# Moving the subtraction that makes the low part of a split weight from GpSimd to VectorE

## Chip, core and metric

The kernel runs on one core of one Trainium2 chip. The metric is the device time of one execution in microseconds (us). Engines are named as the profile names them: PE (TensorE matmul), PEld (TensorE weight load), DVE (VectorE), ACT (ScalarE), POOL (GpSimd), SP (SyncE, which here issues the DMAs).

## What is computed

One step of a two-layer streaming encoder on 2048 prompt frames and 32 sample frames of width 1024. Layer 0 is a sliding-window grouped-query attention with sinks and ALiBi, layer 1 a gated DeltaNet. Cut to what matters here:

```python
for i in range(2):
    h = rmsnorm(x, norm_g[i])
    if i == 0:
        q, k, v, gate = split(h @ attn_w_in)          # 20 blocks of 128 columns
        o = softmax_with_sink(q @ k.T - alibi) @ v    # 64-frame chunks, 128 frames back
        x = x + (o * silu(gate)) @ attn_w_out         # 8 blocks of 128 columns
    else:
        ...                                           # gated DeltaNet: dn_w_in, dn_w_out
y = rmsnorm(x, final_norm_g)
```

All of it is in float32. The projections keep that accuracy on faster matmuls by splitting each operand in two: `hi` is the operand rounded to the type fp32r, `lo` is the operand minus `hi`. A product is then three matmuls: hi·hi, hi·lo and lo·hi.

## The kernel before

**Work and stages.** The tokens lie in four slabs of 512 columns (the second has 544, with the 32 sample frames, and is worked as two groups of 272). In the attention layer each slab goes through 20 blocks of the input projection (`wa`) and 8 of the output projection (`wao`, method `out_blocks`, block number f = 0 to 7). A block is 128 output features: per group of columns 8 input tiles times 3 matmuls, 24 in a row into one bank of the accumulator `pj`, which has two banks. The profile shows this layer from 0 to about 945 us of the span; the DeltaNet layer follows.

**Weights of the attention layer.** Class `Weights` loads a block as two halves (`wr`, 128x512 each, three buffers). `split` then makes, half by half, `hi` by a cast on ACT and `lo` by a subtraction (`low`), each into a tile `wh`. There are six buffers of `wh`, taken in turn; a block uses four of them in the order hi, lo, hi, lo. A new `wh` therefore has to wait until PE has finished with the sixth `wh` before it.

**Weights of the DeltaNet layer.** During the attention of the first two slabs, `keep_ahead` splits all 41 blocks of the later layer once: load half a block (`pr`, two buffers), cast to `ph` on ACT, store `ph` to HBM, subtract in place (`low`), store `pr`. The DeltaNet layer then only loads ready parts (`wh<-xswwd`), so nothing of the change is executed in it.

**Attention.** `attend` handles one pair of heads and 256 frames: scores on PE into two banks `ta`; on DVE the bias is added and the maximum taken (`s<-ta,bias`, `mx`), then three small operations (`mx`, `es`, `mx`); exponentials on ACT; on DVE the sum `den`, its reciprocal and four scalings `s<-s,den`; transposes on PE (`tb`), copies on ACT (`pt`), the product with v on PE (`tc`), the gate on DVE (`of`), and a split of the result (cast on ACT, subtraction on POOL: `hk<-of`).

**Output blocks.** The accumulated block is evacuated by one DVE addition per group, `xr<-pj,xr`, which adds the residual that was loaded into `xr` (two buffers); the sum is stored to HBM.

**Order.** Every instruction is recorded first and issued later by a list scheduler (`Order.flush`). It holds a cost for each operation on each engine (`Estimate.COST`: DVE 68 ns + 1.04 ns an element, POOL 140 + 2.14) and issues on each engine what it believes to be ready, in order of recording. After that the order on each engine is fixed: an engine works its list strictly in order, and an instruction that waits holds up everything behind it. All operations are issued by one helper, so that the profile shows line 185 for each; tiles tell them apart.

Of the kernel before, what the change touches and what calls it, by code (L numbers as in the profile page):

```python
# [12 lines left out]
F32R = mybir.dt.float32r  # L13
# [338 lines left out]
class Weights:  # L352
# [23 lines left out]
    def split(self, free):  # L376
        kern = self.kern
        there = lambda x: free == KT or kern.est.write[x.tensor.name][0] <= kern.clock
        while len(self.lo) < len(self.halves):
            i = len(self.hi)  # L380
            half = self.halves[i if i < len(self.halves) else -1]
            if self.kept is not None:
                if free != KT and free < 4 * i:
                    return
                for made, part in ((self.hi, 0), (self.lo, 1)):
                    made.append(self.place(len(half)))
                    kern.nc.sync.dma_start(
                        made[-1].bitcast(F32), self.kept[half[0] // 4][part][:, half[0] % 4 : half[-1] % 4 + 1, :])
            elif i > len(self.lo) and there(self.hi[-1]):
                self.lo.append(self.place(len(half)))  # L390
                kern.low(self.raws[i - 1], self.hi[-1], self.lo[-1], kern.nc.gpsimd)
            elif i == len(self.lo) and (free == KT or free >= 4 * i) and there(self.raws[i]):
                self.hi.append(self.place(len(half)))
                kern.nc.scalar.copy(self.hi[-1], self.raws[i])
            else:
                return


class Kern:
# [25 lines left out]
    def keep_ahead(self, srcs):  # L425

        nc = self.nc
        todo = [(src, h) for src in srcs for h in range(2)]

        def load(src, h):  # L430
            raw = self.t(self.ap, [P, 4, P], "pr", bufs=2)
            nc.sync.dma_start(raw, self.weight(src)[:, 4 * h : 4 * h + 4, :])
            return raw

        def put(src, h, part, x):
            name = f"w{src[0]}{src[1]}_{h}{part}"
            place = self.dp.tile([P, 4, P], F32, tag=name, name=SCRATCH + name)
            nc.sync.dma_start(place, x)
            return place

        nxt = load(*todo[0])
        for i, (src, h) in enumerate(todo):
            raw, nxt = nxt, load(*todo[i + 1]) if i + 1 < len(todo) else None
            yield raw
            hi = self.t(self.ap, [P, 4, P], "ph", F32R, bufs=1)
            nc.scalar.copy(hi, raw)
            yield hi
            parts = [put(src, h, 0, hi.bitcast(F32))]
            self.low(raw, hi, raw.bitcast(F32R), nc.gpsimd)
            yield raw  # L450
            parts.append(put(src, h, 1, raw))
            self.keeping.setdefault(src, []).append(parts)
            if h:
                self.kept[src] = self.keeping[src]
            yield 4500
# [1797 lines left out]
```

## Time and profile before

| what | before |
|---|---|
| median of 3 runs | 2376.36 us (2372.67 to 2381.98) |
| the profiled execution | 2376.4 us |
| its span, first to last instruction | 2374.6 us |
| mean granted TensorE clock | 0.978 |
| busy in the span: PE, DVE, ACT, POOL | 95%, 69%, 53%, 36% |
| subtractions `wh<-wr,wh` on POOL | 224, 295.5 us |
| subtractions `pr<-pr,ph` on POOL | 82, 111.8 us |

A row of the groups names line, engine, operation, output<-inputs, shapes, count, then busy us and mean ns of one, then the idle time of the engine just before and what ended it. A row of the timeline gives start (us), duration (us), engine, operation, count, and in brackets the idle time before it and who ended that. A row of the windows gives the stretch, its length, the busy us of PE, PEld, DVE, ACT and POOL (with counts), the granted clock, the DMA share and GB/s. A row of the waits says which engine waited before which tile, for whom, for how long in total, how often, and the longest.

### The profile page before, as it was taken

How to read it: one execution, taken by the hardware profiler on the slowest of the kernel's cores; microseconds unless marked ns; L12 is line 12 of the kernel's file. 1: busy time of each engine (PE TensorE's matmuls, PEld its weight loads, DVE VectorE, ACT ScalarE, POOL GpSimd, SP SyncE). 2: the span in 40 equal slices, each digit the busy share in tenths (PEclk: the TensorE clock that was granted, in tenths of full speed). 3: DMA queues.
4: the chain of work that ended last, by engine and by line, in shares of the span. 5: the costliest groups of instructions: out<-in, count | busy, mean ns of one | idle time of the engine just before them, and what ended most of it. 6: DMA issues, size and time to landing. Idle time of an engine off the chain costs nothing.

```text
span 2374.6 us, 44457 instructions
## 1 busy us (share of the span) xinstructions
PE 2252.8 (95%) x14759; PEld 1843.9 (78%) x14759; DVE 1639.6 (69%) x5024; ACT 1262.2 (53%) x3792; POOL 862.9 (36%) x1044
## 2 busy tenths in 40 slices
PE   8998999999999999999999999989999999999997
PEld 5777788797778777777778788877798767777776
DVE  6765465626553445588887768889786888876876
ACT  5555466636553554455566354564644466445533
POOL 4556555665554334222322121331312222122222
PEclk9998999999999999999999999999999999999998
DMA  7556755585434115544423664333456634466442
GB/s 253 175 187 192 255 188 181 174 279 190 147 105 150 62 63 159 193 149 140 143 89 126 200 227 136 128 115 122 147 172 215 200 118 138 134 215 216 155 142 67
DMA packets 222832, 382.75 MB, mean 161 GB/s; under 512 B 29922, under 2 KB 45194, under 8 KB 222602
## 3 DMA queue, kind: packets, MB, share of 16 engines
q1 hardware_dynamic: 220154, 377.75, 49.4%
q8 instruction: 116, 1.90, 0.3%
q10 hardware_dynamic: 2448, 2.16, 0.3%
q14 instruction: 114, 0.93, 0.1%
HBM read 311.63 MB, written 68.19 MB: 160 GB/s over the span
## 4 chain that ended last, share of the span: by engine, by line
PE 56%; DVE 28%; ACT 7%; issue 4%; DMA 3%; POOL 2%; SPq 0%; DVEq 0%; ACTq 0%; POOLq 0%
PE pj L185 39%; PE tb L185 6%; PE ta L185 5%; PE tc L185 4%; DVE cy L185 4%; DVE s L185 3%; DVE sub L185 3%; DVE tl L185 3%; ACT s L185 2%; DVE ml L185 2%; ACT ta L185 1%; DVE xa L185 1%; DVE r L185 1%; DVE md L185 1%; DVE mx L185 1%
## 5 line engine op out<-in xcount | busy, mean ns | idle before, releaser
L185 PE MATMUL pj<-hk,wh 128*128 128x512 f32 (+1 forms) x8184 | 1770.1, 364 | 26.9 <-DVE xr L185 8.6
L185 PEld LDWEIGHTS pj<-hk,wh 128*128 128x128 f32 x8184 | 1326.6, 191 | 237.9 <-issue 14.1
L185 POOL TENSOR_TENSOR wh<-wr,wh 128x512 fp32r<-128x512 f32 x224 | 295.5, 1321 | 328.2 <-ACT wh L185 283.7
L185 DVE SCALAR_TENSOR_TENSOR cy<-cx,cw,cy 128x512 f32<-128x512 f32 x360 | 230.6, 651 | 44.7 <-ACT cy L185 41.1
L185 ACT CAST wh<-wr 128x512 fp32r<-128x512 f32 x224 | 138.1, 618 | 203.6 <-PE pj L185 157.3
L185 ACT ACTIVATE s<-s,mx 128x256 f32<-128x256 f32 (+1 forms) x272 | 132.0, 487 | 30.1 <-DVE mx L185 29.9
L185 ACT ACTIVATE qs<-tb,egq 64x128 f32<-64x128 f32 x264 | 95.7, 362 | 89.7 <-DVE r L185 76.5
L185 DVE TENSOR_TENSOR sub<-ml,tl 128x60 f32<-128x60 f32 (+24 forms) x527 | 125.8, 239 | 10.2
L185 DVE TENSOR_SCALAR s<-s,den 128x256 f32<-128x256 f32 (+1 forms) x272 | 130.9, 530 | 1.2
L185 ACT ACTIVATE cx<-cy 128x512 f32<-128x512 f32 (+1 forms) x96 | 61.1, 636 | 130.9 <-DVE cy L185 101.5
L185 DVE TENSOR_TENSOR tl<-tl,sub 128x60 f32<-128x60 f32 (+24 forms) x527 | 122.3, 232 | 10.1
L185 DVE CUSTOM_DVE_ANT_0 s<-ta,bias 128x256 f32<-128x256 f32 (+1 forms) x272 | 95.7, 405 | 43.5 <-PE ta L185 42.9
L185 POOL TENSOR_TENSOR pr<-pr,ph 128x512 fp32r<-128x512 f32 x82 | 111.8, 1364 | 34.9 <-ACT ph L185 28.8
L185 POOL COPY cx<-hist 128x3 f32<-128x3 f32 x96 | 25.5, 265 | 263.9 <-DVE kq L185 63.6
L185 DVE TENSOR_TENSOR xr<-pj,xr 128x512 f32<-128x512 f32 (+1 forms) x72 | 41.2, 577 | 112.1 <-PE pj L185 70.1
L185 POOL TENSOR_TENSOR so<-so,mhalf 128x4 f32<-128x4 f32 x33 | 36.8, 1115 | 216.9 <-DVE so L185 189.1
L185 DVE SCALAR_TENSOR_TENSOR r<-tb,nbk,vb 64x128 f32<-64x128 f32 x264 | 91.7, 348 | 29.6 <-PE tb L185 25.1
L185 ACT ACTIVATE qs<-o 128x128 f32<-128x128 f32 x132 | 40.7, 308 | 133.8 <-DVE o L185 128.3
L185 ACT COPY cx<-pj 128x512 f32<-128x512 f32 (+2 forms) x149 | 64.1, 445 | 77.5 <-PE pj L185 62.1
L185 PE MATMUL tb<-st,kq 128*128 128x128 f32 x512 | 94.7, 286 | 6.8 <-DVE st L185 5.9
L185 PEld LDWEIGHTS tb<-st,kq 128*128 128x128 f32 x512 | 82.9, 194 | 21.5 <-DVE st L185 13.0
L185 PE MATMUL tb<-con,s 128*128 128x128 f32 (+2 forms) x528 | 77.7, 280 | 18.9 <-DVE s L185 16.0
(242 smaller groups left out, 3558.0 us busy)
## 6 DMA issues: line engine op xcount, KB each, us to landing
wh<-xswwd SPq DMA_DIRECT2D x528, 256.0 KB
wr<-in_wa SPq DMA_DIRECT2D x160, 256.0 KB
wh<-xswwdo SPq DMA_DIRECT2D x112, 256.0 KB
pr<-in_wd SPq DMA_DIRECT2D x66, 256.0 KB
xswwd<-ph SPq DMA_DIRECT2D x66, 256.0 KB
xswwd<-pr SPq DMA_DIRECT2D x66, 256.0 KB
wr<-in_wao SPq DMA_DIRECT2D x64, 256.0 KB
xa<-in_x SPq DMA_DIRECT2D x48, 256.0 KB
```

The lines of the kernel that those rows point to most:

```text
L185: self.order.add(Op(self.name, lambda: call(*args, **kw), cost, op == "dma_start"), ins, outs)
```

## The change

Both calls of `low` on weights name VectorE instead of GpSimd:

```diff
@@ Weights.split
-                kern.low(self.raws[i - 1], self.hi[-1], self.lo[-1], kern.nc.gpsimd)
+                kern.low(self.raws[i - 1], self.hi[-1], self.lo[-1], kern.nc.vector)
@@ Kern.keep_ahead
-            self.low(raw, hi, raw.bitcast(F32R), nc.gpsimd)
+            self.low(raw, hi, raw.bitcast(F32R), nc.vector)
```

`low` itself stays `eng.tensor_tensor(out=lo, in0=src, in1=hi.bitcast(F32), op=ALU.subtract)`. 306 instructions change their engine. The scheduler books them with DVE's cost and orders the attention layer anew on every engine; the DeltaNet layer keeps its order on all of them.

The first place is in slab 0, in an `attend` of the input blocks. On DVE before, its four scalings (`s_245`) and the gate products around them:

```order
L185 TENSOR_TENSOR den_247<-den_247,es_248 128x4
L185 RECIPROCAL den_247<-den_247 128x4
L185 TENSOR_SCALAR s_245<-s_245,den_247 128x256 x4
L185 SCALAR_TENSOR_TENSOR of_272<-tc_269,sg_233 128x256
L185 TENSOR_TENSOR sg_279<-pj_260,rb_169 128x512
L185 SCALAR_TENSOR_TENSOR of_284<-tc_278,sg_233 128x256
```

On POOL before, what stands about the same point:

```order
L185 TENSOR_TENSOR wh_267<-wr_258,wh_261 128x512
L185 TENSOR_TENSOR wh_270<-wr_259,wh_268 128x512
L185 TENSOR_TENSOR pr_314<-pr_314,ph_351 128x512
L185 TENSOR_TENSOR hk_273<-of_272,hk_273 128x256
L185 TENSOR_TENSOR wh_292<-wr_281,wh_285 128x512
```

On DVE now:

```order
L185 TENSOR_TENSOR den_247<-den_247,es_248 128x4
L185 RECIPROCAL den_247<-den_247 128x4
L185 TENSOR_SCALAR s_245<-s_245,den_247 128x256 x4
L185 TENSOR_TENSOR wh_267<-wr_258,wh_262 128x512
L185 TENSOR_TENSOR wh_271<-wr_259,wh_268 128x512
L185 TENSOR_TENSOR pr_314<-pr_314,ph_349 128x512
L185 SCALAR_TENSOR_TENSOR of_272<-tc_270,sg_231 128x256
```

The two subtractions on `wh` and the one on `pr` now stand behind the four scalings, in front of the gate product.

The second place is the output projection of slab 0 (`xr` is the evacuating addition of a block, `acc` a sum of squares). On DVE before, the additions of blocks f = 2, 3 and 4:

```order
L185 TENSOR_TENSOR xr_663<-pj_674,xr_663 128x512
L185 TENSOR_TENSOR acc_665<-acc_665,sq_688 128x512
L185 TENSOR_TENSOR xr_673<-pj_687,xr_673 128x512
L185 TENSOR_TENSOR acc_665<-acc_665,sq_701 128x512
L185 TENSOR_TENSOR xr_686<-pj_700,xr_686 128x512
```

On DVE now, from the addition of block 3 (`xr_663`) to that of block 4 (`xr_674`); `wh_708` and `wh_710` are the low parts of block 6, `wh_721` is that of block 7's first half:

```order
L185 TENSOR_TENSOR xr_663<-pj_675,xr_663 128x512
L185 TENSOR_TENSOR acc_654<-acc_654,sq_689 128x512
L185 TENSOR_TENSOR wh_708<-wr_698,wh_707 128x512
L185 TENSOR_TENSOR pr_831<-pr_831,ph_856 128x512
L185 TENSOR_TENSOR wh_710<-wr_699,wh_709 128x512
L185 TENSOR_TENSOR wh_721<-wr_711,wh_720 128x512
L185 TENSOR_TENSOR xr_674<-pj_688,xr_674 128x512
```

Four subtractions have come between two additions that stood with only an `acc` between them. The tile `wh_721` takes the buffer of the sixth `wh` before it, which is the low part of block 5's second half.

## The prediction, made before the changed kernel was run

> **What bounds the kernel now.** I read the page's busy line first, then the windows by stage, then who PE waits for in the attention layer, then the timeline at its longest waits.
>
> ```profile
> PE 2252.8 (95%) x14759; PEld 1843.9 (78%) x14759; DVE 1639.6 (69%) x5024; ACT 1262.2 (53%) x3792; POOL 862.9 (36%) x1044
> ```
> ```profile
> 0.00:180.00 180.00, 163.50 (x936) 122.28 (x936) 121.71 (x310) 103.42 (x262) 97.08 (x87) 1.00 0.63 203
> 180.00:200.00 20.00, 13.73 (x92) 11.24 (x92) 18.06 (x44) 12.30 (x36) 14.38 (x12) 0.74 0.58 175
> 200.00:220.00 20.00, 17.79 (x114) 15.34 (x114) 8.30 (x15) 11.76 (x30) 11.46 (x10) 0.75 0.54 171
> 220.00:945.00 725.00, 701.74 (x4709) 580.33 (x4708) 375.43 (x1160) 389.00 (x1028) 380.36 (x331) 1.00 0.50 165
> 945.00:2374.00 1429.00, 1356.04 (x8911) 1114.70 (x8909) 1116.09 (x3497) 745.75 (x2438) 359.63 (x607) 0.97 0.48 154
> ```
>
> PE is the bound; no subtraction moves a single matmul away. The change touches only the first 945 us, since the order of the later layer is the same on all engines. There PE is busy 896.8 us (the sum of the first four rows), so 48 us are idle, and the clock column shows about 8 us more lost at 180 to 220 us: (1 - 0.74) x 13.73 + (1 - 0.75) x 17.79. Only these 56 us can be won. DVE is busy 523.5 us of the 945, POOL 503.3.
>
> Who PE waits for in the attention layer:
>
> ```profile
> PE tb L185 <- DVE s L185: 16.0, 20, 2.5
> PE pj L185 <- DVE xr L185: 8.6, 7, 2.0
> PE tc L185 <- ACT pt L185: 6.9, 5, 4.7
> ...
> PE pj L185 <- ACT wh L185: 0.4, 1, 0.4
> ```
>
> The weights themselves are never late (0.4 us). PE waits for the attention chain through DVE (`s`), for the evacuating additions (`xr`), and once for long at `tc`.
>
> **The operation on its new engine.** The groups give the old cost on POOL; DVE's cost is that of its own subtraction of the same shape and inputs, and ACT's cast is needed below:
>
> ```profile
> L185 POOL TENSOR_TENSOR wh<-wr,wh 128x512 fp32r<-128x512 f32 x224 | 295.5, 1321 | 328.2 <-ACT wh L185 283.7
> L185 POOL TENSOR_TENSOR pr<-pr,ph 128x512 fp32r<-128x512 f32 x82 | 111.8, 1364 | 34.9 <-ACT ph L185 28.8
> ```
> ```profile
> L185 DVE TENSOR_TENSOR hk<-xa,hk 128x512 fp32r<-128x512 f32 x8 | 5.4, 680 | 0.7 <-ACT hk L185 0.7
> L185 ACT CAST wh<-wr 128x512 fp32r<-128x512 f32 x224 | 138.1, 618 | 203.6 <-PE pj L185 157.3 <-issue 20.6 <-DMA wr<-in_wa 8.7
> ```
>
> POOL loses 407 us that nobody needs. DVE gets 306 x 0.68 = 208 us, which its 421 idle us of the stage can hold. What matters is where they stand. DVE also gets something back, because its operations stretch beside POOL's subtractions. Timeline of the `attend` of the first order place:
>
> ```profile
> 70.06 4.30 DVE L185 TENSOR_SCALAR s<-s,den 128x256 f32<-128x256 f32 x4
> 70.09 2.58 POOL L185 TENSOR_TENSOR wh<-wr,wh 128x512 fp32r<-128x512 f32 x2 [6.25 <-ACT wh L185]
> 72.64 1.31 POOL L185 TENSOR_TENSOR pr<-pr,ph 128x512 fp32r<-128x512 f32 x1
> 72.88 0.55 PE L185 MATMUL tb<-con,s 128*128 128x128 f32 x3 [0.36 <-DVE s L185]
> 74.25 0.72 PE L185 MATMUL tb<-con,s 128*128 128x128 f32 x4 [0.82 <-DVE s L185]
> ...
> 184.41 0.88 DVE L185 TENSOR_SCALAR s<-s,den 128x256 f32<-128x256 f32 x3
> ```
>
> Three scalings take 0.88 us with POOL quiet; four take 4.30 with three subtractions beside them, and PE waits 0.36 + 0.82 us for them.
>
> **Term 1, the stretch from 172 to 216 us** (the end of slab 0's attention):
>
> ```profile
> 171.90 3.99 DVE L185 TENSOR_SCALAR s<-s,den 128x128 f32<-128x128 f32 x3
> 171.90 1.28 POOL L185 TENSOR_TENSOR wh<-wr,wh 128x512 fp32r<-128x512 f32 x1 [3.09 <-ACT wh L185]
> 173.13 1.30 POOL L185 TENSOR_TENSOR pr<-pr,ph 128x512 fp32r<-128x512 f32 x1
> 174.42 1.32 POOL L185 TENSOR_TENSOR wh<-wr,wh 128x512 fp32r<-128x512 f32 x1
> ...
> 178.65 0.15 DVE L185 TENSOR_TENSOR es<-par,mx 128x4 f32<-128x4 f32 x1
> 184.27 1.60 PE L185 MATMUL tc<-pt,vt 128*64 128x128 f32 x12 [4.68 <-ACT pt L185]
> ...
> 196.79 1.27 POOL L185 TENSOR_TENSOR pr<-pr,ph 128x512 fp32r<-128x512 f32 x1
> 196.88 1.20 DVE L185 TENSOR_TENSOR es<-par,mx 128x4 f32<-128x4 f32 x1
> 198.03 1.26 POOL L185 TENSOR_TENSOR wh<-wr,wh 128x512 fp32r<-128x512 f32 x1
> 198.12 1.19 DVE L185 TENSOR_SCALAR mx<-mx 128x4 f32<-128x4 f32 x1
> 199.65 1.55 PE L185 MATMUL tb<-con,s 128*128 128x128 f32 x6 [2.00 <-DVE s L185]
> ```
>
> `es` and `mx` took 1.20 and 1.19 us instead of about 0.15, which is 2.1 us: the whole of the 2.00 us wait goes. The three `s` were 3.1 us late (3.99 against 0.88); two subtractions now in front of this chain cost it 2 x 0.6 back, so 1.9 of the 4.68 us go. Together -3.9. The half clock follows these two stalls; I give back half of its 8.0: -4.0. Term 1 is -7.9, between 0 (as many subtractions in front of the chain as blocked it) and -14.7 (both waits and the clock whole).
>
> **Term 2, the other waits for `s`:** 16.0 - 2.0 = 14.0 us. The order places the subtractions behind the scalings in most `attend`s, but some in front of them, so I take half: -7, between 0 and -14.
>
> **Term 3, the start.** Low parts enter DVE's first 25 us, where it is nearly full; five cost 3.4 us there, of which the sums beside POOL (below, 0.95 us each instead of 0.68) return a good part: +1, between -1 and +3.
>
> ```profile
> 15.82 4.76 DVE L185 TENSOR_TENSOR acc<-acc,xa 128x512 f32<-128x512 f32 x5
> ```
>
> **Term 4, the output projections.** Here the move adds a wait. DVE's second order place: `wh_721` (block 7) needs the buffer of block 5's last low part, so it cannot run before block 5's last matmul, and `xr_674`, the addition that frees block 4's bank, stands behind it. Block 6 needs that bank. So after block 5's last matmul PE must wait for ACT's cast, DVE's subtraction and DVE's addition. I find the same position eight times: blocks 4, 5, 6 of slab 0 and 3 to 7 of slab 1 (there additions of 272 columns). The rows for the last two links:
>
> ```profile
> 258.42 0.69 DVE L185 TENSOR_TENSOR xr<-pj,xr 128x512 f32<-128x512 f32 x1 [5.63 <-DMA xsx<-xr]
> 259.25 5.79 PE L185 MATMUL pj<-hk,wh 128*128 128x512 f32 x24 [0.72 <-DVE xr L185]
> ...
> 267.02 4.77 PE L185 MATMUL pj<-hk,wh 128*128 128x272 f32 x24 [1.99 <-DVE xr L185]
> ...
> 479.22 0.44 DVE L185 TENSOR_TENSOR xr<-pj,xr 128x272 f32<-128x272 f32 x1 [2.30 <-PE pj L185]
> ```
>
> Price: 0.62 + 0.68 + 0.69 + 0.14 (259.11 to 259.25) = 2.1 us, or 1.9 with the addition of 0.44: 3 x 2.1 + 5 x 1.9 = 15.8. Before, PE already waits 8.6 us for `xr` there, because the residual's load is late (the bracket 5.63); a load that is late anyway covers the new wait, and the larger of the two counts. Term 4 is 15.8 - 8.6 = +7.2, between 0 and 15.8. Queued behind the waiting subtraction on DVE are that addition, the sum `acc` and the next low parts; behind the addition, on SP, the store of `xr` and with it the next load.
>
> **Term 5, the clock after these stalls.** The stall of 1.99 us was followed by this window:
>
> ```profile
> 260.00:280.00 20.00, 16.40 (x100) 14.40 (x99) 5.88 (x18) 6.06 (x15) 8.44 (x8) 0.91 0.75 246
> ```
>
> It lost 0.09 x 16.40 = 1.5 us. The 0.82 us waits at 70 us were followed by none. With three of eight new stalls: +4.5, between 0 and 12. The Trainium skill, page "TensorE: Matmul & The Clock Gate", section "What's actually happening", states that the clock halves after about 3.4 us of idle; this row, after 1.99 us, does not fit it, and by the rule the total would be 2366 (a rival below).
>
> **At no cost.** On SP the stores of `pr` and the loads into `wr` wait for the subtraction:
>
> ```profile
> SPq L185 <- POOL wh L185: 392.4, 178, 7.8
> ```
>
> They move with it, mostly earlier by 1.32 - 0.68 us; PE's 0.4 us wait for weights is the most this can bring, and the loads issued ahead are its cover. If that cover goes, PE waits for weights, which is term 4's kind of price.
>
> **Sum.** -7.9 - 7 + 1 + 7.2 + 4.5 = -2.2 us on the profiled 2376.4, which is also the median (2376.36): 2374 us. A measurement can tell about 0.5%, 11.9 us, from no change.
>
> **Rivals.**
> Faster: the additions' loads are so late that the low parts are long done when they land; the 5.63 us bracket speaks for it, the additions whose wait ended by PE (479.22) against. Terms 4 and 5 vanish: -13.9, 2362.5. Chance 0.30.
> The page's clock rule: short stalls never halve the clock. Term 5 is 0 and all 8.0 us of term 1's clock come back: -2.2 - 4.5 - 4.0 = -10.7, 2366. The 0.91 window speaks against. Chance 0.07.
> Slower: in the two output projections nothing covers the new wait, and every one of the eight stalls halves the clock: 15.8 + 12 - 14.9 + 1 = +13.9, 2390. It decides if PE's gaps there are 1.8 us and more on top of today's and the clock falls under 1.00 behind them. Chance 0.23.
> That the change does nothing is excluded: POOL's list loses 306 instructions.
>
> **How the numbers follow.** The forecast has 0.40; its tails cross the bounds with 0.02 and 0.03. Faster by over 0.5% (under 2364.5): 0.22 of the first rival, 0.03 of the second, 0.02: 0.27. Slower (over 2388.2): 0.23 + 0.03 = 0.26. The rest, 0.35 + 0.08 + 0.04, is 0.47. The range 2355 to 2394 leaves out a quarter of the first rival, the upper part of the slower one and the ends of the bounds. Alone, the forecast has 2364 to 2385.
>
> **What would show it.** Right: PE's wait for `s` falls to about 7 us; four scalings in a row take about 1.2 us; the wait at 184 us shrinks; PE shows gaps near 2 us before `pj`, ended by `xr`, at the eight blocks, with the ACT cast and the DVE subtraction of a `wh` just ahead of the addition; from about 945 us on, the same length as before. Wrong: waits for `s` as long as now, no gaps at the output blocks, or a later layer of another length.

## The result and the profile after

The changed kernel takes 2348.53 us (median of 4 runs, 2343.04 to 2352.12) against 2374.52 us (4 runs of the kernel before in the same comparison): ratio 0.9888, 95% interval 0.9869 to 0.9907. That is 26 us less, where the prediction said 2374 and a range from 2355. The profiled execution took 2349.7 us, its span is 2347.9 us. Below, the busy line of the page after, and then its windows (same columns as before).

```profile
PE 2243.8 (96%) x14759; PEld 1842.6 (78%) x14759; DVE 1724.0 (73%) x5330; ACT 1262.7 (54%) x3792; POOL 467.8 (20%) x738
```
```profile
0.00:25.00 25.00, 18.35 (x70) 14.40 (x71) 15.04 (x24) 15.18 (x25) 1.79 (x7) 1.00 0.84 287
...
0.00:172.00 172.00, 164.95 (x995) 128.39 (x995) 133.22 (x392) 112.07 (x282) 22.47 (x30) 1.00 0.68 222
172.00:216.00 44.00, 40.76 (x244) 33.87 (x243) 29.47 (x64) 23.76 (x58) 7.85 (x8) 1.00 0.69 222
216.00:277.00 61.00, 53.62 (x340) 46.63 (x340) 34.51 (x91) 27.25 (x66) 1.01 (x1) 0.97 0.73 237
277.00:480.00 203.00, 198.80 (x1697) 179.93 (x1693) 140.05 (x471) 122.51 (x355) 31.09 (x37) 1.00 0.61 199
480.00:530.00 50.00, 44.61 (x265) 38.64 (x264) 28.01 (x73) 22.24 (x50) 1.52 (x2) 0.93 0.66 214
530.00:920.00 390.00, 387.62 (x2325) 301.36 (x2324) 244.19 (x747) 208.91 (x546) 44.33 (x57) 1.00 0.40 127
```

PE is busy for 890.4 of the first 920 us (the sum of the six rows from 0:172 to 530:920): 29.6 us idle, for 48.2 before. The half clock at 172 to 216 us is gone (clock 1.00); new dips stand at 216 to 277 and 480 to 530 us. The end of the attention layer is best read from the last additions `xr`. The timeline of tile `xr`, for the kernel before and then the changed one (least, median and greatest duration in ns; then the starts of the first and the last of the eight):

```profile
L185 DVE TENSOR_TENSOR xr<-pj,xr x8: 681/692/692, 913.3 to 948.0; 128x512 f32<-128x512 f32 x8
```
```profile
L185 DVE TENSOR_TENSOR xr<-pj,xr x8: 680/691/692, 887.5 to 922.3; 128x512 f32<-128x512 f32 x8
```

The last starts 25.7 us earlier, so in these two executions the whole gain lies in the attention layer; what follows lasts 1425.6 us (2347.9 - 922.3) for 1426.6 before. Of the 25.7 us, 18.6 are idle time of PE that went (48.2 - 29.6).

Who PE waits for in the layer after, and DVE's groups there. Last, for comparison, the group of the scalings in the kernel before:

```profile
PE pj L185 <- DVE xr L185: 16.3, 10, 1.9
...
PE tb L185 <- DVE s L185: 1.1, 2, 0.9
```
```profile
L185 DVE TENSOR_TENSOR wh<-wr,wh 128x512 fp32r<-128x512 f32 x224 | 159.1, 712 | 139.5 <-ACT wh L185 129.4 <-DMA xswwdo<-pr 2.3 <-PE pj L185 2.2
L185 DVE TENSOR_SCALAR s<-s,den 128x256 f32<-128x256 f32 x240 | 73.0, 357 | 0.9
L185 DVE TENSOR_TENSOR pr<-pr,ph 128x512 fp32r<-128x512 f32 x82 | 58.3, 711 | 4.7 <-ACT ph L185 4.6
```
```profile
L185 DVE TENSOR_SCALAR s<-s,den 128x256 f32<-128x256 f32 x240 | 116.9, 536 | 1.0
```

PE's wait for `s` fell from 16.0 to 1.1 us, its wait for `xr` rose from 8.6 to 16.3, and a scaling takes 357 ns for 536. DVE took over 217.4 us of subtractions (159.1 + 58.3), but its busy time rose only from 1639.6 to 1724.0: 133 us came back from operations that no longer stretch.

Two places of the timeline after. First DVE and POOL in slab 0's last attention steps, then the first of the output blocks that the prediction named (the addition of block 4 in slab 0):

```profile
168.30 1.62 POOL L185 TENSOR_TENSOR hk<-xa,hk 128x544 fp32r<-128x544 f32 x1 [0.86 <-ACT hk L185]
168.64 1.86 DVE L185 SCALAR_TENSOR_TENSOR xa<-xa,par,rb 128x544 f32<-128x544 f32 x1
...
179.26 2.11 DVE L185 TENSOR_SCALAR s<-s,den 128x128 f32<-128x128 f32 x4
179.43 1.34 POOL L185 TENSOR_TENSOR hk<-xa,hk 128x544 fp32r<-128x544 f32 x1 [2.54 <-ACT hk L185]
...
182.39 1.14 DVE L185 TENSOR_SCALAR s<-s,den 128x256 f32<-128x256 f32 x4
...
226.79 0.62 ACT L185 CAST wh<-wr 128x512 fp32r<-128x512 f32 x1 [1.87 <-PE pj L185]
227.44 0.69 DVE L185 TENSOR_TENSOR wh<-wr,wh 128x512 fp32r<-128x512 f32 x1 [1.80 <-ACT wh L185]
228.05 0.68 DVE L185 TENSOR_TENSOR xr<-pj,xr 128x512 f32<-128x512 f32 x1
...
228.88 5.84 PE L185 MATMUL pj<-hk,wh 128*128 128x512 f32 x24 [1.94 <-DVE xr L185]
```

Four larger scalings take 1.14 us with POOL quiet, four smaller ones 2.11 beside one subtraction of POOL's. In the output block the chain is the predicted one: cast, subtraction, addition, and only then the matmuls, after 1.94 us.

### The profile page after: what moved, and what is told of

It reads as the page before. It is cut to its first block, busy times and chain, and to the rows that moved or that the text cites. A ratio compares the mean times of both kernels' runs of the same rounds, so it can differ in the third digit from the quotient of the medians.

```text
span 2347.9 us, 44428 instructions
## 1 busy us (share of the span) xinstructions
PE 2243.8 (96%) x14759; PEld 1842.6 (78%) x14759; DVE 1724.0 (73%) x5330; ACT 1262.7 (54%) x3792; POOL 467.8 (20%) x738
## 3 DMA queue, kind: packets, MB, share of 16 engines
q10 hardware_dynamic: 2448, 2.16, 0.3%
## 4 chain that ended last, share of the span: by engine, by line
PE 66%; DVE 22%; ACT 6%; issue 3%; DMA 1%; POOL 1%; SPq 0%; DVEq 0%; ACTq 0%; POOLq 0%
PE pj L185 47%; PE tb L185 7%; PE ta L185 6%; PE tc L185 4%; DVE cy L185 4%; DVE sub L185 3%; DVE tl L185 3%; ACT ta L185 2%; DVE ml L185 1%; DVE md L185 1%; DVE r L185 1%; PE ms L185 1%; ACT kd L185 1%; DVE st L185 1%; DVE kq L185 1%
## 5 line engine op out<-in xcount | busy, mean ns | idle before, releaser
L185 PE MATMUL pj<-hk,wh 128*128 128x512 f32 (+1 forms) x8184 | 1770.5, 363 | 34.0 <-DVE xr L185 16.3
L185 DVE TENSOR_TENSOR wh<-wr,wh 128x512 fp32r<-128x512 f32 x224 | 159.1, 712 | 139.5 <-ACT wh L185 129.4
L185 POOL TENSOR_TENSOR hk<-of,hk 128x256 fp32r<-128x256 f32 (+1 forms) x72 | 53.4, 742 | 444.8 <-ACT hk L185 439.2
L185 DVE SCALAR_TENSOR_TENSOR st<-st,egl,tc 128x128 f32<-128x128 f32 x128 | 44.3, 346 | 59.4 <-PE tc L185 56.9
L185 ACT COPY pt<-tb 128x512 f32<-128x512 f32 (+2 forms) x144 | 70.6, 528 | 26.4 <-PE tb L185 26.1
L185 DVE TENSOR_SCALAR s<-s,den 128x256 f32<-128x256 f32 (+1 forms) x272 | 81.7, 352 | 1.1
L185 PE MATMUL tc<-pt,vt 128*64 128x128 f32 (+2 forms) x1056 | 79.7, 279 | 1.1 <-DVE of L185 0.6
```

Source lines behind the costliest of these rows:

```text
L185: self.order.add(Op(self.name, lambda: call(*args, **kw), cost, op == "dma_start"), ins, outs)
```

## The experiments

Theory A: POOL's subtractions stretch DVE's operations in the attention chain, and PE waits for that chain. Rival B: the planner's new order gains, whatever engine subtracts. Others formed as results came: C, each new order is a draw; D, what matters in the order is the room that PE has between a step's scores and its transpositions.

All results in one table. "Layer" is the start of the last `xr` addition in the profiled run; "rest" is the span less that. A ratio is to the kernel before in the same comparison.

| run | layer, us | rest, us | median, us | ratio, 95% interval |
|---|---|---|---|---|
| before | 948.0 | 1426.6 | 2372.9 to 2376.6 | |
| changed kernel | 922.3 | 1425.6 | 2348.5 | 0.9869 to 0.9907 |
| e1_only_wh | 941.6 | 1428.0 | 2371.9 | 0.9985 to 1.0006 |
| e2_only_pr | 932.6 | 1421.4 | 2360.9 | 0.9918 to 0.9961 |
| e3_wao_pool | 918.9 | 1432.3 | 2350.0 | 0.9859 to 0.9915 |
| e4_plan_after_pool | 932.6 | 1430.8 | 2359.7 | 0.9924 to 0.9962 |
| e5_plan_before_dve | 933.5 | 1425.8 | 2361.5 | 0.9935 to 0.9973 |
| e6_after_dummy | 990.9 | 1431.8 | 2416.4 | 1.0169 to 1.0211 |
| e7_before_replan | 947.2 | 1431.7 | 2382.9 | 1.0013 to 1.0040 |
| e8_after_replan | 924.4 | 1440.2 | 2361.0 | 0.9922 to 0.9960 |
| e9_before_slack | 938.4 | 1424.9 | 2364.9 | 0.9937 to 0.9969 |
| e10_after_loads320 | 909.9 | 1425.3 | 2338.5 | 0.9809 to 0.9882 |
| e11_after_loads360 | 916.6 | 1427.1 | 2346.3 | 0.9849 to 0.9920 |
| e12_after_both | 898.5 | 1430.0 | 2327.3 | 0.9767 to 0.9825 |
| e13_pool_both | 937.7 | 1425.1 | 2361.2 | 0.9914 to 0.9959 |
| e14_after_slack | 922.8 | 1425.3 | 2348.8 | 0.9860 to 0.9910 |
| e15_both_on_pool | 918.4 | 1425.7 | 2348.6 | 0.9857 to 0.9908 |
| e16_xa_too | 893.4 | 1421.6 | 2318.4 | 0.9742 to 0.9771 |
| e17_xa_of_too | 894.1 | 1417.9 | 2320.3 | 0.9746 to 0.9792 |

The rest differs by 14 us between kernels although the DeltaNet layer's order is the same in all of them but e7 and e8. So the layer's end says more about an edit in the attention layer than the median does, and the two are read together. But each layer value comes from one execution, and how far it scatters between executions was not measured: differences of a few us in it are not safe.

### The engine and the order taken apart

The change does two things: another engine subtracts, and the planner, which counts that, makes another order on all engines. `Engine` joins a name for the planner and an engine for the work, so each can be changed alone. e4 keeps the changed order and lets POOL work; e5 keeps the old order (PE's, ACT's and SP's lists are the old ones, instruction for instruction) and lets DVE work.

```diff
 # e4 (e5: Engine("gpsimd", nc.vector, est, order)), beside the loop in Engines
+        self.low = Engine("vector", nc.gpsimd, est, order)
...
-                kern.low(self.raws[i - 1], self.hi[-1], self.lo[-1], kern.nc.vector)
+                kern.low(self.raws[i - 1], self.hi[-1], self.lo[-1], kern.nc.low)
...
-            self.low(raw, hi, raw.bitcast(F32R), nc.vector)
+            self.low(raw, hi, raw.bitcast(F32R), nc.low)
```

Expected of e4:

> The order of work that the planner made for subtractions on DVE, with POOL doing them at their places. Theory A: s goes back to about 530 ns, PE's waits for s to 14 to 20 us and the half clock at 172 to 216 us comes back; the xr additions no longer stand behind a subtraction on their own engine, so the eight stalls shrink to about the old 8.6 us. Time 2366 to 2380 us, near the kernel before. Theory B (the order is what gains): at or under the changed kernel, 2335 to 2350 us.

Expected of e5:

> The order of work that the planner made for subtractions on POOL, with DVE doing them at the places where they stood in the list of all engines. Theory A: s at about 360 ns, PE's waits for s under 4 us, no half clock at 172 to 216 us; the output blocks decide the rest: 2338 to 2356 us. Theory B: the old order loses, 2368 to 2382 us.

Measured: -15.4 us in the layer for the order alone (e4) and -14.5 for the engine alone (e5). Waits and scalings of e4, then of e5:

```profile
PE tb L185 <- DVE s L185: 6.6, 14, 0.9
```
```profile
L185 DVE TENSOR_SCALAR s<-s,den 128x256 f32<-128x256 f32 x240 | 119.9, 551 | 1.0
```
```profile
PE pj L185 <- DVE xr L185: 15.5, 9, 2.5
...
PE tb L185 <- DVE s L185: 4.9, 6, 1.3
```
```profile
L185 DVE TENSOR_SCALAR s<-s,den 128x256 f32<-128x256 f32 x240 | 77.1, 365 | 0.9
```

In e4 the scalings are as slow as before (551 ns), as A says, but PE waits only 6.6 us for them instead of 16.0. Neither theory had that. In e5 the scalings are fast and PE's wait for `s` falls in the old order too, while the output stalls are there (15.5). Each change alone gives about half of the gain: some 15 us of 25.7 in the layer, 13 and 11 of 26 in the median. The layers add up to 29.9 us, more than both together give; the medians add up to 24.6, a little less than 26.0. So it is not shown that the two overlap. A is right for about half of the gain, B for the other half.

### Work beside DVE put back

e6 is the changed kernel with a further subtraction on POOL for each of the 306, reading `hi` twice, its result read by nobody.

```diff
+class Both:
...
+    def tensor_tensor(self, out, in0, in1, op):
+        self.nc.gpsimd.tensor_tensor(out=self.scr[:, : in1.free_size()].rearrange("p (a b) -> p a b", b=P), in0=in1, in1=in1, op=op)
+        self.nc.vector.tensor_tensor(out=out, in0=in0, in1=in1, op=op)
```

> The changed kernel with its order on DVE, and for each of the 306 subtractions an extra one on POOL that reads the same high part and whose result (bfloat16, to a tile of its own) nobody reads. Only the work beside DVE is put back. Theory A: s back to 500 to 540 ns, PE's waits for s to 14 to 20 us, the half clock at 172 to 216 us back, the eight output stalls as in the changed kernel or longer: 2370 to 2388 us, as slow as before or slower. Theory B (order, or a subtraction of 0.7 instead of 1.3 us, is what gains): 2345 to 2353 us, no difference from the changed kernel.

Measured: 2416.4 us, 68 above the changed kernel, beyond the expected range. DVE's groups in the first 945 us, and its timeline beside POOL:

```profile
L203 DVE TENSOR_TENSOR wh<-wr,wh 128x512 fp32r<-128x512 f32 x212 | 179.6, 849 | 113.2 <-ACT wh L185 107.4 <-PE pj L185 2.4 <-DMA xa<-in_x 1.1
L185 DVE TENSOR_SCALAR s<-s,den 128x256 f32<-128x256 f32 x236 | 104.2, 493 | 0.9
L203 DVE TENSOR_TENSOR pr<-pr,ph 128x512 fp32r<-128x512 f32 x82 | 83.8, 1022 | 6.3 <-ACT ph L185 6.2
```
```profile
68.41 1.04 POOL L202 TENSOR_TENSOR scr<-ph 128x512 bf16<-128x512 f32 x1 [1.08 <-ACT ph L185]
...
68.48 0.41 DVE L185 CUSTOM_DVE_ANT_0 s<-ta,bias 128x256 f32<-128x256 f32 x1
...
73.27 2.71 DVE L185 TENSOR_SCALAR s<-s,den 128x256 f32<-128x256 f32 x4
73.37 2.46 POOL L202 TENSOR_TENSOR scr<-wh 128x512 bf16<-128x512 f32 x2 [3.92 <-ACT wh L185]
```

Nobody reads the result of POOL's extra work, and still the scalings went from 357 to 493 ns and four of them to 2.71 us. So POOL working beside DVE stretches DVE's operations; that is shown. How much of the 68 us comes from it is not, for the extra subtraction also reads `hi`: ACT's next cast into that buffer must wait until POOL is done, and did so for 21.3 us.

```profile
ACT wh L185 <- POOL scr L202: 21.3, 11, 4.2
```

What was underrated is that DVE's own subtractions stretch too, from 712 to 849 and 1022 ns. The operation on scores (`s<-ta,bias`, one input from PSUM) keeps its 0.41 us beside POOL. The Trainium skill, page "SBUF — State Buffer", section "Who interferes with whom", states this division: a DVE operation with two SBUF inputs, or in a 2-port mode, and a GpSimd operation that reads SBUF exclude each other, and the second waits for the first; the trace agrees in these rows.

### One call at a time

```diff
 # e1: pr back on POOL
-            self.low(raw, hi, raw.bitcast(F32R), nc.vector)
+            self.low(raw, hi, raw.bitcast(F32R), nc.gpsimd)
 # e2: wh back on POOL
-                kern.low(self.raws[i - 1], self.hi[-1], self.lo[-1], kern.nc.vector)
+                kern.low(self.raws[i - 1], self.hi[-1], self.lo[-1], kern.nc.gpsimd)
```

> Only the 224 subtractions of wh go to DVE; the 82 of pr stay on POOL. Theory A (POOL's subtractions stretch the DVE operations of the attention chain): POOL keeps 82 x 1.36 = 112 of 407 us of such work, and one pr stands in each of the two waits at 172 to 200 us, so most but not all of the gain: 2352 to 2360 us, s at 400 to 430 ns a scaling, PE's wait for s at 3 to 6 us; the eight stalls of the output blocks stay, since they come from wh alone. Theory B (the planner's new order brought the gain, whatever engine subtracts): nothing follows from the number of subtractions on POOL, s may stay near 530 ns while the time falls.

> Only the 82 subtractions of pr go to DVE; the 224 of wh stay on POOL. The first four runs left theory A (POOL's subtractions stretch DVE's operations) with half of the gain, and the order that the planner makes with the other half. Theory A in proportion: POOL loses 82 x 1.36 = 112 of 407 us of work, about a quarter; no new stall at the output blocks, since no wh subtraction stands on DVE: 2362 to 2370 us, s at 480 to 520 ns, PE's wait for xr near the old 8.6 us. Theory C (each new order is a draw, good or bad by chance, and moves the time by 10 us whatever the engine): the time has no relation to the share, 2352 to 2380 us.

e1 missed: no change in the median, -6.4 us in the layer, although 224 of 306 subtractions moved. e2 gives -15.4 in the layer with the other 82. The gain does not go by number. PE's waits and the scalings in e1, then PE's wait for `s` in e2:

```profile
PE pj L185 <- DVE xr L185: 14.4, 9, 1.9
...
PE tb L185 <- DVE s L185: 1.2, 2, 0.7
```
```profile
L185 DVE TENSOR_SCALAR s<-s,den 128x256 f32<-128x256 f32 x240 | 75.3, 366 | 1.1
```
```profile
PE tb L185 <- DVE s L185: 6.8, 12, 1.0
```

The subtractions of `wh` carry the output stalls with them (14.4 us against 8.6 before), those of `pr` don't (5.9). The wait for `s` does not explain the two runs. In e1 it falls to 1.2 us and a scaling to 366 ns, as in the changed kernel, and the median does not move; in e2 a scaling still takes 507 ns, the wait is 6.8 us, and 15 us are gained in the layer and in the median. So short waits for `s` are not yet a gain. The layer of e1 is 19.3 us longer than that of the changed kernel: PE is idle for 36 us of it instead of 30, some 7 us more are lost to half-clock stretches (six instead of three, one of them double), and the rest lies in PE's busy time. Why the order made for e1 costs that much is not settled, and neither is why 82 subtractions of `pr` are worth that much: the room that is counted below is in e2 that of the kernel before, and in the prediction's term 1 one of them stands beside DVE in each of the two waits. The two gains add up to 21.8 of 25.7 us in the layer, and to 16 of 26 us in the median.

### Is a new order a draw?

e7 and e8 change one number of the planner in both kernels, so that a new order comes out for the same engines:

```diff
-    COST = {"vector": (68, 1.04, 60), "scalar": (52, 0.83, 93), "gpsimd": (140, 2.14, 0)}
+    COST = {"vector": (68, 1.04, 60), "scalar": (52, 0.83, 93), "gpsimd": (140, 2.30, 0)}
```

> The kernel before, with only the planner's cost of GpSimd operations raised by a thirteenth (2.30 ns an element for 2.14, which is nearer to the 1.32 us measured): a new order, no engine changed. Theory C (a re-planned order moves the time by chance): 5 to 15 us away from before, on either side. Otherwise, if orders made for the same engines are worth the same: 2368 to 2377 us.

> The changed kernel with the same small change to the planner's cost of GpSimd operations: a new order, the same engines. Theory C: 5 to 15 us away from the changed kernel, 2335 to 2363 us. Otherwise 2344 to 2353 us, with the output stalls as in the changed kernel.

In the attention layer they came to -0.8 and +2.1 us. So these two orders, each made for the same engines as the one that it is compared with, are worth the same within some 2 us there. That speaks against C for the 15 us of e4, but two draws do not exclude it: below, e11 differs from e10 by one number of the planner, and by 6.7 us in the layer. The medians are 7 and 12 us worse. This number plans the DeltaNet layer too, and the rest of e8 (1440.2 us) lies outside what the other kernels show; that of e7 (1431.7 us) does not.

### Room between scores and transpositions

What is better in the new order? I counted in PE's list, for each of the 72 steps, the matmuls between its last score (`ta`) and its first transposition (`tb`), at the planner's own durations (216 ns for 512 columns, 116 for 272, 110 for the rest):

```
order                     mean room   steps with less than 8 us
before, e5                7.88 us     41 of 72
changed kernel, e4        8.55 us     26 of 72
e1                        8.16 us     44 of 72
e2                        7.86 us     39 of 72
e7                        8.0  us     37 of 72
e8                        8.6  us     27 of 72
e9                        9.30 us      7 of 72
e10                       9.3  us     16 of 72
e11                       8.8  us     21 of 72
e12, e15                 10.11 us      9 of 72
```

The planner counts 0.6 us for a subtraction on DVE; where one stands beside a softmax, it presumably plans the transpositions later, so that PE gets other matmuls in between. The orders of e7 and e8, which were worth the same as those that they are compared with, have nearly the same room as well. e9 gives the kernel before such room by telling the planner how long a scaling really takes there:

```diff
-            each = 0.52
+            each = 1.6 if out.tensor.name.startswith("s_") else 0.52
```

> The kernel before, POOL subtracting, with one number of the planner changed: it counts a scaling of s at 1.6 ns an element for 0.52 (537 ns for 128x256, the 536 ns that the trace of before shows, instead of 261). By the order, PE then does 9.3 us of other matmuls between a step's last score matmul and its first transposition, for 7.9 before and 8.55 in the order of the changed kernel. Theory D (half of the gain is this room, which the planner leaves because it counts the subtractions on DVE): the attention layer ends at 928 to 938 us instead of 948.7, PE's waits for s fall to 7 us or less with s still at 530 to 560 ns: 2355 to 2364 us. Rival (room is not what counts; the order made for DVE helps by something else, such as when weights are split): layer at 945 to 951 us, 2369 to 2378 us.

```profile
PE tb L185 <- DVE s L185: 2.4, 5, 0.7
```
```profile
L185 DVE TENSOR_SCALAR s<-s,den 128x256 f32<-128x256 f32 x240 | 131.6, 594 | 0.9
```

Scalings slower than ever (594 ns), and PE waits 2.4 us for them instead of 16.0. The layer falls by 9.6 us, a little short of what D expected (10 to 20), and short of e4's 15.4. Room alone gives most of what the order gave; that it is all of it is not shown, and e2, which gains without more room, speaks against it.

e14 gives the changed kernel more room the same way (1.0 in place of 1.6):

> The changed kernel with only the scaling of s counted at 1.0 ns an element: 9.5 us of room for 8.55, the eight (here nine) places of the output projections kept. Theory D says that room is worth the waits for s that are left, 1.1 us, and the waits at 178 and 253 us at most: layer at 918 to 923 us, 2341 to 2349 us, waits for xr at 15 to 18 us. If more room is worth more by itself: under 915 us.

```profile
PE pj L185 <- DVE xr L185: 16.0, 10, 1.9
```

As expected, nothing: +0.5 us in the layer. Behind the eight stalls more room buys nothing.

### The output stalls

e3 leaves the 64 subtractions of the output weights on POOL. e10 and e11 keep all on DVE and let the planner count loads faster in the attention layer; then it expects the residual sooner, and lists the addition `xr` ahead of the subtraction that waits for a buffer (one of the eight places left with 320, none with 360).

```diff
 # e3
-                kern.low(self.raws[i - 1], self.hi[-1], self.lo[-1], kern.nc.vector)
+                kern.low(self.raws[i - 1], self.hi[-1], self.lo[-1], kern.nc.gpsimd if self.src[0] == "wao" else kern.nc.vector)
 # e10 (e11: 360); back to 250 ahead of the DeltaNet layer
-        self.last = 0.0
+        self.last, self.rate = 0.0, 320
...
-            self.free["dma"] = max(start + 1500, self.at("dma")) + n / 250
+            self.free["dma"] = max(start + 1500, self.at("dma")) + n / self.rate
...
-            cost = n / 250
+            cost = n / self.rate
```

> As the changed kernel, but the 64 subtractions of wh for the output projections' weights (wao) stay on POOL; 160 of wh and all of pr are on DVE. If the eight stalls of 1.8 to 1.94 us are what the subtraction in front of the xr addition costs, seven or eight of them go, with the three half-clock stretches behind them: 8 x 1.85 + 3 x 1.7 = 20 us gross, less 6 to 8.6 us that PE waits for xr in any case: 2334 to 2342 us, PE's wait for xr at 5 to 10 us. If another link (late loads, the chain of buffers) holds PE there in any case: 2345 to 2352 us with the same gaps. Theory C: 2338 to 2362 us, no relation to the gaps.

> The changed kernel, but in the attention layer the planner counts loads at 320 bytes per ns for 250; so it expects the residual's load sooner and lists the xr additions ahead of the subtractions that wait for a buffer. By the order one of the eight output stalls is left, and one other place arises (a gate product behind a subtraction). If the order in front of xr is what costs the stalls: the waits for xr fall from 16.3 to 4 to 9 us and the attention layer ends at 908 to 917 us instead of 923.0: 2333 to 2343 us. If the residual's loads hold PE there in any case (as the run with wao on POOL began to show): layer at 919 to 924 us, 2344 to 2352 us.

> As the run before with 360 bytes per ns: by the order none of the eight places is left. Order in front of xr as the cause: layer at 906 to 916 us, waits for xr at 3 to 9 us, 2331 to 2342 us. Loads as the cause: 919 to 924 us, 2344 to 2352 us, the same waits for xr as in the run with 320.

PE's wait for `xr` in e3 and in e10:

```profile
PE pj L185 <- DVE xr L185: 11.9, 8, 2.5
```
```profile
PE pj L185 <- DVE xr L185: 0.3, 1, 0.3
```

e3 missed: only -3.4 us against the changed kernel in the layer, and nothing in the median. Its order was new as well, two stalls of 1.8 us stayed and others of 2.54, 2.16 and 1.49 us took the place of the rest. In e10 the wait is gone (0.3 us): -12.4 us in the layer, some 11 in the median. So the order in front of `xr`, not the residual's load, held PE there. At most about 12 us of the 16.3 come back, and perhaps not all of them for this reason, since the order of e10 has more room too (9.3 us for 8.55). e11 has no such stall either but gives only -5.7; it has waits of 2.27 and 2.79 us elsewhere and less room than e10, and which of these costs the difference is open.

### Both, and the engine under a good order

e12 joins e10 with 1.0 ns an element for the scalings. e13 gives the kernel before the same help (320, and 1.6), with POOL subtracting and the planner knowing it. e15 is e12's order with POOL subtracting, made as in e4.

> The changed kernel with loads at 320 and a scaling of s at 1.0 ns an element (384 ns; the changed kernel's trace shows 357): none of the eight places by the order, and 10.1 us of matmuls between a step's scores and its transpositions for 8.55. Waits for s are already 1.1 us, so more room gains at most those and the waits of 0.5 to 1.6 us for other links; it can lose at the end of each slab, where there is nothing to fill the room. Theory D: layer within 3 us of the run with 320 or 360, 2330 to 2343 us. If room is worth more than the waits for s show: under 905 us.

> The kernel before (POOL subtracts, and the planner knows it) with loads counted at 320 bytes per ns and a scaling of s at 1.6 ns an element: by the order 9.6 us of room for 7.9. If the change's gain is mostly the order, this kernel without the change comes near the best one: layer at 903 to 915 us, 2327 to 2342 us. If work beside DVE counts as much (theory A and D, each about half): layer at 915 to 935 us, 2340 to 2360 us.

> The order of the best kernel (loads 320, s 1.0, planned for DVE), with POOL doing the subtractions: the engine alone, under a good order. Theory A: s at 530 to 560 ns, acc and xa longer too; the room of 10.1 us hides much of it, waits for s at 2 to 6 us: layer at 905 to 918 us against 899.2, 2333 to 2348 us. If under a good order the engine no longer matters: layer at 897 to 903 us, 2325 to 2332 us.

The windows of e12, and waits and scalings of e15:

```profile
0.00:895.00 895.00, 879.88 (x5847) 726.25 (x5848) 616.99 (x1833) 519.33 (x1354) 107.15 (x132) 1.00 0.56 182
```
```profile
PE tb L185 <- DVE s L185: 2.7, 5, 0.9
```
```profile
L185 DVE TENSOR_SCALAR s<-s,den 128x256 f32<-128x256 f32 x240 | 112.0, 515 | 1.2
```

e12 takes 2327.3 us, faster than both kernels; PE is idle for 15.1 of its first 895 us. It went 11.4 us under e10, where D had expected 3: D's point that room is worth only the waits for `s` falls here, for e10's wait was 1.9 us. What else the new order brought is open. e15 against e12 is the engine alone under a good order: +19.9 us in the layer, +21.3 in the median. So the engine goes on counting, at least as much as in the old order (14.5 us in the layer, 11 in the median). e13 reaches only 937.7: with these two numbers at least, planning better does not replace moving the subtractions.

### The rest of POOL's subtractions

The timeline after still showed POOL's `hk<-xa` beside stretched DVE operations. e16 moves these to DVE in e12, e17 also the 72 of `hk<-of`.

```diff
 # e16 and e17
-                    self.low(o.x[k - 1], h[:, 0, :n], h[:, 1, :n], nc.vector if gcol else nc.gpsimd)
+                    self.low(o.x[k - 1], h[:, 0, :n], h[:, 1, :n], nc.vector)
 # e17 only
-        self.split(of[:, :n], og(i, 0)[:, ocol : ocol + n], og(i, 1)[:, ocol : ocol + n], nc.gpsimd)
+        self.split(of[:, :n], og(i, 0)[:, ocol : ocol + n], og(i, 1)[:, ocol : ocol + n], nc.vector)
```

> The best kernel so far (subtractions on DVE, loads 320, s 1.0) with the 24 subtractions hk<-xa of the later slabs' inputs on DVE too. In the trace of the changed kernel these are the POOL work beside which DVE still stretches (an xa product of 1.86 us for 0.77, an es of 1.30 for 0.16, at 168 to 176 us). Theory A: s falls under 360 ns, but only 15.1 us of idle time is left on PE in the layer, 6.1 of it at the start: layer 894 to 900 us, 2320 to 2329 us. If a limit is reached where DVE's own load counts: layer over 902 us, 2330 us or more.

> As the run before, with the subtractions hk<-of of the attention's outputs (72 of them) on DVE as well, so that POOL reads next to nothing in the layer. Theory A alone: s at its undisturbed 290 ns, layer 892 to 900 us, 2318 to 2329 us. If DVE's own load counts (these stand in the chain from tc to the output projection): layer over 902 us, 2330 us or more.

The windows and the scalings of e17, and then all its scalings by tile (least, median and greatest duration in ns, then the first and the last start):

```profile
0.00:895.00 895.00, 881.66 (x5866) 725.53 (x5867) 627.58 (x1933) 519.08 (x1355) 21.88 (x39) 1.00 0.56 183
```
```profile
L185 DVE TENSOR_SCALAR s<-s,den 128x256 f32<-128x256 f32 x240 | 72.2, 348 | 0.7
```
```profile
L185 DVE TENSOR_SCALAR s<-s,den x272: 278/348/361, 46.9 to 852.1; 128x256 f32<-128x256 f32 x120, 128x128 f32<-128x128 f32 x8, 32x160 f32<-32x160 f32 x8
```

The layer shortens by 5.1 and 4.4 us against e12, as A expects, though the planner made a new order here as well and the two were not taken apart. DVE's own load is no limit yet, and POOL has 21.9 us of work left in e17. No scaling stretches any more: the longest takes 361 ns, in the kernel before 1482. The expected 290 ns was a misreading, not a stretch left over: it is the busy time of a row of scalings by their number, in which each starts before the last has ended, and 348 ns is also the median of a single one in the kernel before. e16 is the fastest kernel, 2318.4 us; e17's interval overlaps with it.

## Why the prediction was wrong

The forecast was -2.2 us in sum. Its mechanisms are all in the trace; it failed in the steps that halved the gain.

**Term 1** said -7.9 and measured -13.7. The row of the kernel before for this stretch is

```profile
172.00:216.00 44.00, 35.12 (x215) 28.60 (x214) 34.36 (x73) 24.38 (x66) 28.76 (x23) 0.77 0.53 166
```

so idle fell from 8.9 to 3.2 us (-5.6; the same stretch of time, though PE is a little further in its list now), and the 8.1 us lost to the half clock, (1 - 0.77) x 35.12, came back whole. "I give back half of its 8.0" and "two subtractions now in front of this chain cost it 2 x 0.6 back" were the failed steps.

**Term 2**, "some in front of them, so I take half", is the largest error by a little. Forecast -7; of 14 us of waits for `s` outside that stretch about 1 is left, so -13. The count from DVE's list was right, but the list of PE had changed as well: it leaves more room. e4 shows the new order alone (PE's wait for `s` from 16.0 to 6.6 with unchanged scalings), and e5 the other (to 4.9 in the old order). Either of them takes away more than the 2.0 + 7 us that I granted to both. I had read DVE's order only, and compared where subtractions stood in it. (That the wait falls is not the whole gain, as e1 shows: there it falls as far, and the median does not.)

**Term 3** said +1 for the start. PE was busy 18.35 us of the first 25 against 16.55 before: -1.8, the wrong sign.

**Term 4** was right in place and size. The eight gaps are 1.94, 1.94 and 1.89 us in slab 0 and five of 1.80 in slab 1 (forecast 2.1 and 1.9), and the wait for `xr` grew by 7.7 (forecast 7.2). e10 shows that what hides behind them is more: 12.4 us.

**Term 5** said three half-clock stretches, +4.5. Windows of the changed kernel:

```profile
238.00:241.40 3.40, 3.40 (x10) 2.65 (x9) 0.17 (x1) 0.83 (x2) 0.00 (x0) 0.50 0.62 204
...
483.80:487.20 3.40, 3.40 (x18) 3.40 (x17) 1.33 (x2) 0.98 (x2) 0.00 (x0) 0.50 0.92 296
494.00:497.40 3.40, 3.40 (x17) 3.40 (x17) 1.19 (x2) 0.33 (x1) 0.00 (x0) 0.50 0.99 304
```

Three it is, but "three of eight" had no working behind it and came true by luck: which of the stalls are followed goes by where they fall (last section). They lose 4.7 us by the windows ((1 - 0.97) x 53.62 + (1 - 0.93) x 44.61), of which the dip of 1.5 us at 260 to 280 us of the kernel before must be taken off, which the term forgot: +3.2.

**The sum.** -5.6 - 13 - 1.8 + 7.7 make -12.7 of the 18.6 us of idle that went; the other 5.9 are waits that the forecast left alone, above all those for `pt`, behind the same scalings (2.2 us at `tc` beside the 4.68 that are in term 1, and 2.7 at `tb`). With the clock, -8.1 + 3.2, it is -23.5 of 25.7; the rest is within PE's busy time.

**The rivals.** "Terms 4 and 5 vanish" was wrong: the additions did stand in wait. (The bracket of 5.63 us that spoke for it names the store `xsx<-xr`, not the load; that the load was late was inferred.) The clock rule was wrong here: three stalls of 1.80 to 1.94 us were followed by a half clock. The slower case had its condition met by half: there are eight gaps of 1.8 us and more, but the wait for `xr` grew by 7.7 us and not by 15.8, three of them and not eight met the clock, and the gain was larger. That the DeltaNet layer would keep its length was right (1425.6 for 1426.6).

## What to carry to other kernels

When a planner sets the order, an edit to one engine's work changes every engine's list: compare the lists of the engine that waits too, here how much other work PE has between handing over a step and wanting it back. A vector operation with slow stretches shows what it could be by its quietest rows; where those stretches all stand beside another engine's work, moving that work can give the difference back on every one of them, as it did for the scalings in e17, and a forecast should halve it only for a reason it can show. What the shorter operations are then worth in time is another question: e1 had them and gained nothing. Then look behind the gain for the new wait: here a subtraction that waits for a buffer, queued ahead of an addition that frees a bank, took back up to 12 us that a change in the planner's load rate returned.

## What the runs showed of the hardware beyond what was expected

POOL's subtraction of 128x512 took 1321 ns, DVE's 680 to 712. Work on POOL that nobody reads stretched DVE's two-input subtractions from 712 to 849 and 1022 ns and the scalings from 357 to 493, while the operation that reads one input from PSUM kept 0.41 us.

The clock halved for 3.4 us after stalls of 1.80 to 1.94 us, in three of eight cases. The Trainium skill, page "TensorE: Matmul & The Clock Gate", section "What's actually happening", speaks of an idle window of about 3.4 us; the trace does not agree.

Which stalls are followed can be read from where the half-clock stretches start. In the changed kernel 238.0, 483.8 and 494.0 us are 72 and 3 steps of 3.413 us apart; in the kernel before 182.8, 199.9 and 268.1 us are 5 and 20 such steps apart, and in all 19 traces the distances are whole numbers of this step. The three stalls that were followed lie whole in one step (1.94, 1.80 and 1.80 us). Of the other five, three are cut by the end of a step into parts of 1.23 us and less, and two leave 1.63 and 1.79 us in one. In the kernel before a stall of 2.45 us, cut into 1.37 and 1.08, was followed by nothing. In the attention layers of all traces, each of the 32 steps at full clock with more than 1.83 us of idle time on PE was followed by a half clock; below that some were and some were not, and why is open. So a stall of 2 us may cost a half-clock stretch or not, by where it falls.

The same DeltaNet instructions in the same order took from 1417.9 to 1432.3 us in the profiled runs of different kernels. The windows of this rest in e2 and in e3:

```profile
932.60:2354.00 1421.40, 1349.51 (x8898) 1108.60 (x8896) 1113.62 (x3497) 745.79 (x2438) 361.95 (x606) 0.97 0.49 154
```
```profile
918.90:2351.00 1432.10, 1359.29 (x8898) 1119.16 (x8896) 1115.48 (x3497) 746.33 (x2438) 360.52 (x606) 0.96 0.48 153
```

The same 8898 matmuls keep PE busy for 9.8 us longer in e3, which is most of the 10.7 us between the two, and the mean clock is lower (0.96 for 0.97). What decides how often the clock dips there stays open.
